# Eight kinds of small TensorE work start only when the last of them has its data: a two-layer encoder on one core

## The chip, the cores and the metric

One core of a Trainium2 chip runs the kernel. Its engines work side by side, each through its own instructions in a fixed order: TensorE (PE in the profile; its weight loads are PEld) multiplies matrices into PSUM, VectorE (DVE) and ScalarE (ACT) do elementwise work, and SyncE (SP) issues the transfers from memory. The metric is the device time of one execution in microseconds (us), as the median of several runs.

## The reference

Two layers work on x of 256 tokens by 2048 channels, in float32. Cut to what matters:

```python
shift, scale, gate = split(c @ w_ada + b_ada, 3)
h = rms_norm(x, g_pre) * (1 + scale) + shift
u, g_pool, q, k, v, g_diff = split(h @ w_in)            # 2048 -> 6144, six parts of 1024
pool = (trailing_mean(u, 2|4|8|16) - u) @ w_pool * pool_scale * silu(g_pool)   # 4 groups of 256
q, k = rotary(q), rotary(k)                              # 8 heads, 2 maps of 64 each
a = softmax(mask(q1 k1')) - lam * softmax(mask(q2 k2'))  # chunk-causal
diff = rms_norm(a @ v, subln_g) * (1 - lam_init) * silu(g_diff)
y = concat(pool, diff) @ w_out                           # 2048 -> 2048
x = x + (1 + gate) * rms_norm(y, g_post)
```

## The kernel before

**The two big products.** `h @ w_in` and `concat @ w_out` make up nearly all of TensorE's work. Each weight is split in two parts of lower precision, `whi` (a CAST on ACT) and `wlo` (the rest, a subtraction on DVE), and so is the activation (`hi` and `lo`). A product is the sum of three matmuls of 128x512: hi·whi, hi·wlo, lo·whi. In the profile these are the matmuls `accc<-whiz,hz`, `accc<-wloz,hz` and the same with `catz`; they are called the main matmuls below. A unit is one 256x512 piece of a weight: twelve main matmuls, six for each of its two 128-row halves. The tokens stand in two tiles of 128 (`st` 0 and 1). The order of the units, and so of all main matmuls, is laid out once in `plan` and `lay_out` (lines 438 and after) and does not depend on the scheduler.

**The small TensorE work.** Between the main matmuls TensorE does transposes and small products, all into PSUM tiles `psb`:

- `make_h` (line 912): for each 256 channels of a layer's input, ACT or DVE scales the two token tiles (`xn`, a `halfz` tile), four transposes of 128x128 turn them, and ACT and DVE write `hi` and `lo` (`hz`), which the main matmuls of w_in read.
- `rope` (line 1135): four transposes for each token tile of a finished q or k block.
- `head` and `heads` (lines 1163 and 1190): the score products of one head; the transposes of its softmax weights; the products with v; and four transposes of a pair of heads' gated result, which ACT and DVE turn into `catz`, read by the main matmuls of w_out.
- `pool_group` (line 1283): the products with a band matrix, and those with w_pool.

**What sets the order.** The program is written as many tasks (threads), one for each such piece of work; the main matmuls are a task of their own. Each instruction of a task asks for its engine, and a planner (`Flow`) picks which asking instruction is put on its engine next. It keeps a clock of its own for each engine and, for each tile, when it was written and last used. `depends` (line 276) gives the time at which all that an instruction reads is written. `next_of` (line 208) takes, among the instructions that could begin by now, the one with the earliest due time; the main matmuls have the latest due time of all, so any small TensorE instruction whose inputs have been ready long enough goes ahead of them. "Long enough" is `SLACK`, 1.5 us after its inputs are written (line 145); this counts for small TensorE work alone. When the task of the main matmuls waits for an `hz` or `catz` tile that no instruction makes yet, it does not ask, and TensorE gets whatever asks.

All this is settled while the program is built. On the chip each engine runs its list in order, and an instruction waits only for the tiles that it really reads or overwrites. So four transposes of one group are put on TensorE one by one: if the first two tiles are ready earlier than the last, main matmuls come between them.

`halfz`, `zz`, `yz`, `rawz`, `adaz` are tiles in SBUF (half tiles, block results, raw weights, rows of w_ada). Every instruction is recorded by one helper, so the profile shows line 126 for all of them; the tile names tell them apart.

Of the kernel before, what the change touches and what calls it, by code (L numbers as in the profile page):

```python
# [23 lines left out]
P = 128  # L24
# [59 lines left out]
class Task:  # L84
# [2 lines left out]

    def __init__(self, flow, f, due):
        self.flow, self.f, self.due = flow, f, due
        self.ask, self.cond, self.error, self.over = None, None, None, False  # L90
        self.go = threading.Semaphore(0)
        self.thread = threading.Thread(target=self.run, daemon=True)
        self.thread.start()
# [37 lines left out]
class Flow:  # L131
# [37 lines left out]

    def due(self, due):  # L170
        self.cur.due = due if callable(due) else lambda: due

    def resume(self, t):
        self.cur = t
# [73 lines left out]
    def turn(self, key, op, outs, ins, total, table):  # L248

        a = Ask()  # L250
        size = lambda x: math.prod(x.shape[1:])
        a.key, a.op, a.table, a.dma = key, op, table, "dma" in op
        a.bytes = 4 * size(outs[0]) * outs[0].shape[0]
        outs, ins = ([x for x in xs if not x.tensor.name.startswith(("in_", "out_"))] for xs in (outs, ins))
        a.outs, a.ins = [self.region(x) for x in outs], [self.region(x) for x in ins]
        a.names = {r[0] for r in a.outs + a.ins}
        a.dep, a.f32 = None, key == "tensor" and op == "matmul" and ins[-1].dtype == F32
        if a.dma:
            a.us = 0.35
        elif key == "tensor":  # L260
            n, dt = size(outs[0]), ins[-1].dtype
            if op == "transpose":
                a.us = 0.109
            elif dt == F32:
                a.us = max(0.109, 0.835e-3 * n) * (1 if ins[0].shape[0] == DQK else 2)
            else:
                a.us = 0.0135 + 0.4167e-3 * n if dt == F32R else 0.08
        else:
            fixed, each, accum, _ = self.COST[key]
            a.us = fixed + each * max(size(x) for x in outs + ins) + total * accum  # L270
            if key == "scalar":
                a.us += 0.07 * (len(ins) - 1)
        self.cur.ask = a
        self.pause()

    def depends(self, a):
        t = 0.0
        for r in a.ins:
            t = max(t, self.latest(self.wrote, r))
            if a.key != "tensor" and r[0].startswith(("acc", "ps")):  # L280
                t = max(t, self.latest(self.used, r))
        for r in a.outs:
            if a.key != "tensor" or not self.wrote.get(r[0]):
                t = max(t, self.latest(self.used, r))
        return t

    def note(self, a):
# [111 lines left out]
class Kern:  # L399
# [512 lines left out]
    def make_h(self, l, kp):  # L912

        nc, f = self.nc, self.f
        early = kp < self.START[l]

        f.wait(lambda: self.gated[l - 1][0] >= 2 and self.made[l] > 2 * kp + bool(early) if l else early or self.made[l] > 2 * kp)
        t, hi, lo = self.two("h")
        self.h[l, kp] = t, hi, lo
        if early:  # L920
            for st in range(NST):
                f.spawn(lambda st=st: self.half_h(l, kp, st, hi, lo), 2.0 * st + 0.1 * kp - 3.9 if l else st + 0.1 * kp - 5.5)
            return
        f.wait(lambda: all(r is not None for r in self.xr[l]))
        xn = self.tmp.take([P, NST, S], "xn")
        for st in range(NST):
            self.scaled(xn[:, st, :], self.x[st][:, kp * S : (kp + 1) * S], self.xr[l][st])
        b = self.bank()
        for i in range(2):
            for st in range(NST):  # L930
                nc.tensor.transpose(b[:, i * S + st * P : i * S + (st + 1) * P], xn[:, st, i * P : (i + 1) * P], self.ident)
        self.tmp.give(xn)
        hf = self.tmp.take([P, 2, S], "hf")
        for i in range(2):
            kt = 2 * kp + i
# [199 lines left out]
    def rope(self, l, nb, acc):  # L1135

        nc, v, f, z = self.nc, self.nc.vector, self.f, self.z[l, nb]
# [15 lines left out]
            rot.append(t1)  # L1153
        for st in range(NST):
            b, r = self.bank(), rot[st].rearrange("p g e d -> p (g e d)")
            for h in range(4):
                nc.tensor.transpose(b[:, h * P : (h + 1) * P], r[:, h * P : (h + 1) * P], self.ident)
            self.tmp.give(rot[st])
            self.copy(z[:, st, :], b)
            self.banks.give(b)  # L1160
        self.turning -= 1

    def head(self, l, h0, qT, kT, st, p):

        nc, v = self.nc, self.nc.vector
        c = slice(h0 * P, (h0 + 1) * P)
        nm, s = st[:, 0:4], st[:, 4:8]

        maps = [(m, slice(m * DQK, (m + 1) * DQK)) for m in range(2)]
        bank = self.banks.take([P, 512], "ps", n=2)  # L1170

        for t, o in ((0, slice(0, P)), (1, slice(P, 3 * P))):
            for m, r in maps:
# [16 lines left out]
    def heads(self, l, hp):  # L1190
# [34 lines left out]
        aT = []  # L1225
        for h in range(2):
            b = self.bank()
            for t in range(2):
                for j in range(t + 1):
                    nc.tensor.transpose(b[:, (t + j) * P : (t + j + 1) * P], p[h][t][:, 0, j * P : (j + 1) * P], self.ident)  # L1230
            if h == 0:
                self.tmp.give(tiles[0])
            a = self.tmp.take([P, 3, P], "aT")
            self.copy(a.rearrange("p i q -> p (i q)"), b[:, 0 : 3 * P])
            self.banks.give(b)
            aT.append(a)
        self.tmp.give(*tiles[1:])
        av = self.bank()
        for h in range(2):
            hs = slice((h0 + h) * P, (h0 + h + 1) * P)  # L1240
            o = av[:, 2 * h * P : (2 * h + 1) * P]
# [25 lines left out]

        cat, hi, lo = self.two("cat")
        b = self.bank()
        for i in range(2):  # L1270
            for st in range(NST):
                nc.tensor.transpose(
                    b[:, i * S + st * P : i * S + (st + 1) * P], gz[:, st, (h0 + i) * P : (h0 + i + 1) * P], self.ident
                )
# [8 lines left out]
    def pool_group(self, l, g):  # L1283
# [3 lines left out]
        u, gp = self.z[l, U[half]], self.z[l, GP[half]]  # L1287
        f.wait(lambda: self.band is not None and self.wps[l] is not None)
        b = self.bank()
        for ct in range(2):  # L1290
            c = slice((2 * gg + ct) * P, (2 * gg + ct + 1) * P)
            o = b[:, ct * S : (ct + 1) * S]
# [6 lines left out]
        self.copy(pt.rearrange("p c s -> p (c s)"), b)  # L1299
        self.banks.give(b)  # L1300
        m = self.bank()
        for dt in range(2):
            for ct in range(2):
                nc.tensor.matmul(
# [118 lines left out]
```

## Time and profile before

| what | value |
|---|---|
| median of 3 runs | 829.72 us (828.36 to 830.87) |
| the profiled execution | 828.36 us, of which the profile's span is 826.6 us |
| TensorE busy | 800.4 us, 97% of the span; 4058 matmuls |
| VectorE, ScalarE busy | 699.9 us (85%), 543.4 us (66%) |
| TensorE's granted clock | 0.996 of full speed over the span |
| HBM | 242.17 MB read, 296 GB/s over the span |

How to read what is quoted later: a row of the timeline gives start, length in us, engine, instruction, what it writes and reads, shapes and how often it stands there in a row; in brackets the idle time of the engine before it and what ended that idle time. Matmuls overlap each other, so the pitch of two matmuls is the difference of their starts, and not their length. A float32 matmul that is not a transpose has two records.

### The profile page before, as it was taken

The page shows a single profiled execution, that of the slowest core. Times are in us where ns is not written, and L with a number is a line of the kernel's source. Part 1 is how long each engine was busy: PE and PEld are TensorE (multiplying, and loading weights), DVE is VectorE, ACT ScalarE, POOL GpSimd, SP SyncE. Part 2 cuts the span into 40 slices and gives each one's busy share as a digit, 9 for nine tenths or more (in the row PEclk, how much of TensorE's full clock was granted, in tenths as well). Part 3 has the DMA queues.
Part 4 walks back from the last instruction along what each step waited for, and adds up shares of the span by engine and source line. Part 5 has one row for each costly group of instructions (what it writes and reads, how often), then busy time and mean ns, then how long its engine had stood idle before and what let it go on. Part 6 is the DMA issues. An engine that isn't in the chain of part 4 may idle for free.

```text
span 826.6 us, 11859 instructions
## 1 busy us (share of the span) xinstructions
PE 800.4 (97%) x4058; PEld 662.0 (80%) x4058; DVE 699.9 (85%) x1258; ACT 543.4 (66%) x944; POOL 0.2 (0%) x4
## 2 busy tenths in 40 slices
PE   4899999999999999999999999999999999999995
PEld 1688789888998877778878889888898887778884
DVE  7988998989989889888999979879788997678814
ACT  4879999967656666667387657576565466677520
POOL 0000000000000000000000000000000000000000
PEclk9999999999999999999999999999999999999998
DMA  9999999799999776876997899999999973545403
GB/s 344 407 409 409 408 408 334 277 357 380 364 404 337 262 237 204 300 230 209 313 340 264 312 338 360 341 357 364 330 404 374 380 256 112 183 142 170 134 0 102
DMA packets 68382, 245.07 MB, mean 296 GB/s; under 512 B 7745, under 2 KB 8033, under 8 KB 68065
## 3 DMA queue, kind: packets, MB, share of 16 engines
q1 hardware_dynamic: 68034, 244.14, 80.8%
q8 instruction: 32, 0.52, 0.3%
q10 hardware_dynamic: 288, 0.17, 0.1%
q14 instruction: 28, 0.23, 0.1%
HBM read 242.17 MB, written 2.11 MB: 296 GB/s over the span
## 4 chain that ended last, share of the span: by engine, by line
PE 94%; DVE 3%; ACT 2%; issue 0%; DMA 0%; DVEq 0%; ACTq 0%
PE accc L126 84%; PE psb L126 10%; DVE adaz L126 1%; ACT sqj L126 0%; ACT hz L126 0%; DVE x L126 0%; DVE rh L126 0%; DVE wloz L126 0%; DVE ry L126 0%; ACT zz L126 0%; PE accb L126 0%; ACT halfz L126 0%; ACT junkz L126 0%; DMA cb<-in_c 0%; ACT accc L126 0%
## 5 line engine op out<-in xcount | busy, mean ns | idle before, releaser
L126 PE MATMUL accc<-whiz,hz 128*128 128x512 f32 x1272 | 403.3, 394 | 7.6 <-ACT hz L126 5.3
L126 ACT CAST whiz<-rawz 128x1024 fp32r<-128x1024 f32 (+1 forms) x259 | 263.7, 1045 | 100.1 <-DMA rawz<-in_w_in 52.4
L126 DVE TENSOR_TENSOR wloz<-rawz,whiz 128x1024 fp32r<-128x1024 f32 (+1 forms) x259 | 307.2, 1207 | 14.3 <-ACT whiz L126 12.8
L126 PEld LDWEIGHTS accc<-whiz,hz 128*128 128x128 f32 x1272 | 237.9, 188 | 63.4 <-ACT hz L126 7.0
L126 DVE SCALAR_TENSOR_TENSOR adaz<-adaz,cb 128x1024 f32<-128x1024 f32 x192 | 231.5, 1220 | 30.3 <-DMA adaz<-in_w_ada 29.4
L126 PE MATMUL accc<-wloz,hz 128*128 128x512 f32 x636 | 249.6, 393 | 0.0
L126 PE MATMUL accc<-whiz,catz 128*128 128x512 f32 x512 | 165.7, 399 | 0.5 <-ACT catz L126 0.3
L126 PEld LDWEIGHTS accc<-wloz,hz 128*128 128x128 f32 x636 | 119.8, 188 | 24.6 <-DVE wloz L126 0.5
L126 PEld LDWEIGHTS accc<-whiz,catz 128*128 128x128 f32 x512 | 94.9, 188 | 20.7 <-ACT catz L126 0.7
L126 PE MATMUL accc<-wloz,catz 128*128 128x512 f32 x256 | 101.6, 397 | 0.0
L126 ACT COPY zz<-accc 128x512 f32<-128x512 f32 x128 | 73.9, 589 | 24.2 <-PE accc L126 23.6
L126 ACT COPY accc<-zz 128x512 f32<-128x512 f32 x110 | 65.1, 593 | 24.8 <-DVE halfz L126 17.8
L126 PE MATMUL accc<-hz,whiz 128*128 128x256 f32 x512 | 72.5, 284 | 0.0
L126 PEld LDWEIGHTS accc<-hz,whiz 128*128 128x128 f32 x512 | 66.7, 192 | 0.7
L126 PEld LDWEIGHTS accc<-wloz,catz 128*128 128x128 f32 x256 | 48.1, 188 | 10.4 <-issue 0.8
L126 PE MATMUL accc<-hz,wloz 128*128 128x256 f32 x256 | 41.2, 283 | 0.0
L126 ACT ACTIVATE sqj<-accc 128x512 bf16<-128x512 f32 x16 | 9.6, 600 | 41.0 <-PE accc L126 40.8
L126 PE MATMUL psb<-consts,halfz 128*128 128x128 f32 x176 | 30.6, 277 | 5.6 <-ACT halfz L126 5.6
L126 PEld LDWEIGHTS accc<-hz,wloz 128*128 128x128 f32 x256 | 35.3, 192 | 0.0
L126 DVE TENSOR_TENSOR yz<-accc,Gz 128x512 f32<-128x512 f32 x16 | 11.0, 690 | 27.8 <-ACT sqj L126 27.6
L126 PEld LDWEIGHTS psb<-consts,halfz 128*128 128x128 f32 x176 | 22.2, 142 | 14.1 <-ACT halfz L126 8.1
L126 ACT ACTIVATE halfz<-psb,sm 128x128 f32<-128x128 f32 (+1 forms) x64 | 26.4, 420 | 9.9 <-DVE sm L126 6.0
(108 smaller groups left out, 505.8 us busy)
## 6 DMA issues: line engine op xcount, KB each, us to landing
adaz<-in_w_ada SPq DMA_DIRECT2D x192, 512.0 KB, 7.1
rawz<-in_w_in SPq DMA_DIRECT2D x189, 512.0 KB, 7.1
rawz<-in_w_out SPq DMA_DIRECT2D x64, 512.0 KB, 4.2
x<-in_x SPq DMA_DIRECT2D x2, 1024.0 KB, 8.8
wpz<-in_w_pool SPq DMA_DIRECT2D x4, 512.0 KB, 7.2
Gz<-gate SPq DMA_DIRECT2D x4, 512.0 KB, 5.7
out<-x SPq DMA_DIRECT2D x8, 256.0 KB, 2.8
rawz<-in_w_in SPq DMA_DIRECT2D x6, 256.0 KB, 8.8
```

The source lines that it names most:

```text
L126: return f(*args, **kw)
```

## The change

The planner gets a call `until(*tiles)`: the next instruction of the task is held, in the planner's eyes, until these tiles are written too (`also`, read in `depends`). Eight places call it just before the first instruction of a group, with the tiles that the group's later instructions read: the four transposes of `make_h`, of `rope` and of a head pair's result, the score products, the transposes of the softmax weights, the products with v, and both products of a pool group. Nothing is added on the chip; no instruction and no wait is new. What changes is the order in which instructions are put on the engines, and with it which buffers they get.

```diff
--- before.py
+++ after.py
@@ -169,6 +169,10 @@
+    def until(self, *tiles):
+
+        self.cur.also = [self.region(x) for x in tiles]
@@ -253,7 +257,8 @@
         a.outs, a.ins = [self.region(x) for x in outs], [self.region(x) for x in ins]
-        a.names = {r[0] for r in a.outs + a.ins}
+        a.also, self.cur.also = self.cur.also, []
+        a.names = {r[0] for r in a.outs + a.ins + a.also}
@@ -282,6 +287,8 @@
             if a.key != "tensor" or not self.wrote.get(r[0]):
                 t = max(t, self.latest(self.used, r))
+        for r in a.also:
+            t = max(t, self.latest(self.wrote, r))
         return t
@@ -926,6 +933,7 @@
         b = self.bank()
+        f.until(xn)
         for i in range(2):
             for st in range(NST):
                 nc.tensor.transpose(b[:, i * S + st * P : i * S + (st + 1) * P], xn[:, st, i * P : (i + 1) * P], self.ident)
@@ -1153,6 +1161,7 @@
             b, r = self.bank(), rot[st].rearrange("p g e d -> p (g e d)")
+            f.until(r)
@@ -1162,12 +1171,13 @@
         bank = self.banks.take([P, 512], "ps", n=2)
+        f.until(qT, kT)
@@ -1225,6 +1235,7 @@
             b = self.bank()
+            f.until(*(p[h][t][:, 0, :] for t in range(2)))
@@ -1236,6 +1247,7 @@
         av = self.bank()
+        f.until(*aT, vz)
@@ -1267,6 +1279,7 @@
         b = self.bank()
+        f.until(gz[:, :, h0 * P : (h0 + 2) * P])
@@ -1287,6 +1300,7 @@
         b = self.bank()
+        f.until(u)
@@ -1303,6 +1313,7 @@
         m = self.bank()
+        f.until(pt)
```

Both programs have the same 3878 TensorE instructions. In the order before, main matmuls are interrupted by small work 114 times (from one instruction to eighteen at a time); in the changed order 93 times. Three places in detail, each as the order before and the changed order.

**First place: layer 0, the fourth h tile.** TensorE's order. `psb` is what the transposes of `make_h` write; `hz_1119` before and `hz_1142` now is the new h tile, and the matmuls above it read an older one. Before, one transpose of the group stands nine main matmuls higher up:

```order
L126 MATMUL accc_1128<-wloz_1095,hz_895 128x512
L126 MATMUL psb_1147<-consts_80,halfz_1120 128x128 x3
L126 MATMUL accc_1128<-whiz_1065,hz_895 128x512
L126 MATMUL accc_1139<-whiz_1065,hz_895 128x512
L126 MATMUL accc_1139<-wloz_1095,hz_895 128x512
L126 MATMUL accc_1139<-whiz_1065,hz_895 128x512
L126 MATMUL accc_1128<-whiz_1094,hz_1119 128x512
L126 MATMUL accc_1128<-wloz_1155,hz_1119 128x512
L126 MATMUL accc_1128<-whiz_1094,hz_1119 128x512
```

Now:

```order
L126 MATMUL accc_1145<-wloz_1078,hz_884 128x512
L126 MATMUL accc_1145<-whiz_1060,hz_884 128x512
L126 MATMUL psb_1157<-consts_80,halfz_1143 128x128 x4
L126 MATMUL accc_1130<-whiz_1070,hz_1142 128x512
L126 MATMUL accc_1130<-wloz_1101,hz_1142 128x512
L126 MATMUL accc_1130<-whiz_1070,hz_1142 128x512
L126 MATMUL accc_1145<-whiz_1070,hz_1142 128x512
L126 MATMUL accc_1145<-wloz_1101,hz_1142 128x512
```

Before, four main matmuls stand between the last transposes and the first matmul that reads the new tile. Now all four transposes stand together, directly ahead of that matmul.

ScalarE's order at the same place; `hz` is the rounded `hi` of each half of the new tile, `halfz` the unrounded value from which VectorE makes `lo`. Before:

```order
L126 ACTIVATE hz_1119<-psb_1147,AB_90 128x256
L126 ACTIVATE halfz_1171<-psb_1147,AB_90 128x256
L126 COPY zz_377<-accc_1099 128x512
L126 ACTIVATE hz_1119<-psb_1147,AB_90 128x256
L126 ACTIVATE halfz_1171<-psb_1147,AB_90 128x256
```

Now:

```order
L126 ACTIVATE hz_1142<-psb_1157,AB_90 128x256
L126 ACTIVATE halfz_1180<-psb_1157,AB_90 128x256
L126 CAST whiz_1136<-rawz_937 128x1024
L126 ACTIVATE hz_1142<-psb_1157,AB_90 128x256
L126 ACTIVATE halfz_1180<-psb_1157,AB_90 128x256
```

Between the first and the second half of the tile there was a COPY, and now there is a CAST of a weight.

**Second place: layer 0, the last pair of heads.** TensorE's order. `psb` is the transposed result of the pair, from which ScalarE and VectorE make `catz_3819` before and `catz_3834` now. Before:

```order
L126 MATMUL psb_3820<-consts_80,zz_527 128x128
L126 MATMUL accc_3249<-whiz_3463,catz_3675 128x512
L126 MATMUL psb_3820<-consts_80,zz_527 128x128 x2
L126 MATMUL accc_3249<-wloz_3491,catz_3675 128x512
L126 MATMUL psb_3820<-consts_80,zz_527 128x128
L126 MATMUL accc_3249<-whiz_3463,catz_3675 128x512
L126 MATMUL accc_3242<-whiz_3490,catz_3763 128x512
L126 MATMUL accc_3242<-wloz_3524,catz_3763 128x512
L126 MATMUL accc_3242<-whiz_3490,catz_3763 128x512
```

After these rows nine more matmuls read `catz_3763`, and the next reads `catz_3819`: thirteen main matmuls lie between the last transpose and the first use. Now:

```order
L126 MATMUL accc_3242<-whiz_3495,catz_3714 128x512
L126 MATMUL accc_3242<-wloz_3515,catz_3714 128x512
L126 MATMUL accc_3242<-whiz_3495,catz_3714 128x512
L126 MATMUL psb_3835<-consts_80,zz_527 128x128 x4
L126 MATMUL accc_3238<-whiz_3514,catz_3834 128x512
L126 MATMUL accc_3238<-wloz_3537,catz_3834 128x512
L126 MATMUL accc_3238<-whiz_3514,catz_3834 128x512
L126 MATMUL accc_3242<-whiz_3514,catz_3834 128x512
```

The four transposes stand together and directly ahead of the first matmul that reads what is made of them.

**Third place: layer 1, a change of accumulators near the end of w_in.** TensorE's order. `accc_6854` before and `accc_6844` now is an accumulator that is first filled by a COPY from an earlier sum. Before:

```order
L126 MATMUL accc_6801<-wloz_6569,hz_5698 128x512
L126 MATMUL accc_6801<-whiz_6554,hz_5698 128x512
L126 MATMUL psb_6849<-consts_80,halfz_6758 128x128 x4
L126 MATMUL psb_6862<-consts_80,halfz_6758 128x128 x4
L126 MATMUL accc_6854<-whiz_6567,hz_5698 128x512
L126 MATMUL accc_6854<-wloz_6577,hz_5698 128x512
L126 MATMUL accc_6854<-whiz_6567,hz_5698 128x512
```

Now:

```order
L126 MATMUL accc_6802<-wloz_6552,hz_5702 128x512
L126 MATMUL accc_6802<-whiz_6543,hz_5702 128x512
L126 MATMUL accc_6844<-whiz_6563,hz_5702 128x512
L126 MATMUL accc_6844<-wloz_6566,hz_5702 128x512
L126 MATMUL accc_6844<-whiz_6563,hz_5702 128x512
L126 MATMUL accc_6849<-whiz_6563,hz_5702 128x512
```

The eight transposes of a rotated block that stood ahead of the new accumulator's first matmul have moved to a later place. ScalarE's order there; before (the fill of `accc_6854` was a COPY on VectorE):

```order
L126 COPY zz_4823<-accc_6779 128x512
L126 COPY zz_4675<-psb_6849 128x512
L126 COPY zz_4675<-psb_6862 128x512
L126 COPY accc_6864<-zz_4895 128x512
L126 CAST whiz_6852<-rawz_6744 128x1024
```

Now:

```order
L126 COPY zz_4820<-accc_6774 128x512
L126 COPY accc_6844<-zz_4892 128x512
L126 COPY zz_4820<-accc_6802 128x512
L126 COPY accc_6849<-zz_4892 128x512
L126 CAST whiz_6842<-rawz_6777 128x1024
```

Both fills are now on ScalarE, in turn with the COPYs that empty the two accumulators before them.

More of the change, by code (lines that the diff above doesn't have):

```diff
@@ L89, in __init__ @@
         self.flow, self.f, self.due = flow, f, due
-        self.ask, self.cond, self.error, self.over = None, None, None, False
+        self.ask, self.cond, self.error, self.over, self.also = None, None, None, False, []
         self.go = threading.Semaphore(0)
@@ L1163, in head @@
     def head(self, l, h0, qT, kT, st, p):
-        nc, v = self.nc, self.nc.vector
+        nc, v, f = self.nc, self.nc.vector, self.f
         c = slice(h0 * P, (h0 + 1) * P)
```

## The prediction

> **What bounds the kernel now.** I read the page first (its engines and its chain), then the stretches of the span one by one, then the timeline at each place where TensorE waits.
>
> ```profile
> span 826.6 us, 11859 instructions
> PE 800.4 (97%) x4058; PEld 662.0 (80%) x4058; DVE 699.9 (85%) x1258; ACT 543.4 (66%) x944; POOL 0.2 (0%) x4
> PE 94%; DVE 3%; ACT 2%; issue 0%; DMA 0%; DVEq 0%; ACTq 0%
> ```
>
> TensorE sets the end: 97% busy, and 94% of the chain. Busy time does not tell where its 26 idle us lie, so the span is cut at the places where TensorE stops:
>
> ```profile
> 0.00:32.00 32.00, 18.25 (x40) 9.36 (x41) 24.91 (x87) 16.83 (x29) 0.20 (x4) 1.00 0.95 366
> 32.00:303.00 271.00, 270.20 (x1402) 228.88 (x1400) 246.39 (x365) 208.26 (x312) 0.00 (x0) 1.00 0.94 356
> 303.00:323.00 20.00, 19.28 (x98) 14.74 (x99) 16.58 (x34) 13.81 (x29) 0.00 (x0) 1.00 0.70 237
> 323.00:422.00 99.00, 99.00 (x500) 79.58 (x499) 89.16 (x216) 61.89 (x152) 0.00 (x0) 1.00 0.76 258
> 422.00:437.00 15.00, 14.18 (x63) 10.86 (x62) 13.98 (x35) 14.11 (x33) 0.00 (x0) 1.00 0.84 333
> 437.00:705.00 268.00, 268.00 (x1410) 228.94 (x1409) 233.79 (x345) 168.20 (x248) 0.00 (x0) 1.00 0.89 326
> 705.00:709.00 4.00, 3.65 (x20) 2.69 (x19) 2.73 (x7) 2.90 (x5) 0.00 (x0) 1.00 0.00 0
> 777.00:817.00 40.00, 39.88 (x177) 32.66 (x175) 12.52 (x23) 9.78 (x22) 0.00 (x0) 1.00 0.08 27
> ```
>
> The columns after each stretch are its length, then busy time and count of TensorE, its weight loads, VectorE, ScalarE and GpSimd, then granted clock, transfers' share and GB/s. Nearly all idle time lies in the first 32 us and after TensorE's last matmul at 817, and the change moves nothing there: by the order, the first TensorE instruction that moves is one that runs near 54 us, and behind the last moved transposes the main matmuls stand as before. Between 32 and 817 us TensorE is idle for some 2.7 us in all (0.80, 0.72, 0.82, 0.35 in the rows shown with gaps). So **what this change can win from waits is under 3 us; what it can lose has no such limit.** The last row gives the pitch of a main matmul, 39.88 / 177 = 0.225 us.
>
> **Part one: fewer interruptions.** A group taken apart, and one that stands whole:
>
> ```profile
> 85.20 0.40 PE L126 MATMUL accc<-wloz,hz 128*128 128x512 f32 x1
> 85.43 0.39 PE L126 MATMUL accc<-whiz,hz 128*128 128x512 f32 x1
> 85.66 0.27 PE L126 MATMUL psb<-consts,halfz 128*128 128x128 f32 x1
> 85.69 0.48 PE L126 MATMUL accc<-whiz,hz 128*128 128x512 f32 x1
> 86.01 0.49 PE L126 MATMUL psb<-consts,halfz 128*128 128x128 f32 x3
> 86.25 0.48 PE L126 MATMUL accc<-wloz,hz 128*128 128x512 f32 x1
> 86.57 0.39 PE L126 MATMUL accc<-whiz,hz 128*128 128x512 f32 x1
> ...
> 263.15 0.60 PE L126 MATMUL psb<-consts,halfz 128*128 128x128 f32 x4
> 263.51 0.48 PE L126 MATMUL accc<-wloz,hz 128*128 128x512 f32 x1
> 263.82 0.63 PE L126 MATMUL accc<-whiz,hz 128*128 128x512 f32 x2
> ```
>
> The whole group holds up the main matmuls by 0.36 us (263.15 to 263.51), and the matmul after it takes 0.31 us to the next instead of 0.225: 0.44 in all, 0.11 a transpose. Taken apart as one and three: from 85.20 to 86.57 it is 1.37 us, in which four main matmuls begin (4 x 0.225 = 0.90), so 0.47. Putting a group together is worth some 0.025 us. The order has 114 interruptions before and 93 after: 21 x 0.025 = **-0.5 us**. Bounds: nothing, or the whole late matmul saved each time, 21 x 0.085 = -1.8. I stay at the low end, since the two cases above are direct measurements of the exchange.
>
> [...]
>
> **Part two: groups that now stand directly ahead of their reader.** This is where I expect the loss. The wait in the planner's eyes holds the first transposes back until the last tile is written plus its 1.5 us of slack. Where that moment is late, the group drops down to the first main matmul that needs its result, and everything from the transpose to the written tile lies open. Behind the waiting main matmul all TensorE work is queued.
>
> First place (fourth h tile of layer 0). Before:
>
> ```profile
> 111.68 0.49 PE L126 MATMUL psb<-consts,halfz 128*128 128x128 f32 x3
> 112.20 0.57 ACT L126 ACTIVATE hz<-psb,AB 128x256 fp32r<-128x256 f32 x1 [0.95 <-PE psb L126]
> 113.17 0.40 PE L126 MATMUL accc<-wloz,hz 128*128 128x512 f32 x1
> 113.26 0.43 DVE L126 TENSOR_TENSOR hz<-halfz,hz 128x256 fp32r<-128x256 f32 x1 [0.57 <-ACT halfz L126]
> 113.74 0.74 PE L126 MATMUL accc<-whiz,hz 128*128 128x512 f32 x2 [0.18 <-DVE hz L126]
> 114.32 0.40 PE L126 MATMUL accc<-wloz,hz 128*128 128x512 f32 x1
> ```
>
> From the start of the three transposes the `hi` half is written 112.77 - 111.68 = 1.09 us later, and the matmul that reads `lo` starts 2.06 us later. A fourth transpose adds 0.11 to both: 1.20 and 2.17. Before, four main matmuls covered the first of these and the wait was for `lo` alone: 113.17 to 113.74 is 0.57, less 0.225, so 0.34, and the matmul after a wait is 0.11 late as well (113.74 to 114.32 is 0.58 for two). Now, counted from the group's start: without a wait the main matmuls go on at 0.36; they go on at 1.20, a loss of 0.84 and 0.11. The third of them, which reads `lo`, could start at 1.20 + 0.34 + 0.225 = 1.77 and waits until 2.17: 0.40 and 0.11. Together 1.46, less the 0.45 lost there before, less the 0.085 that follows any group: +0.9. Then the second half: ScalarE has a CAST ahead of it where it had a COPY of 0.59 us:
>
> ```profile
> L126 ACT CAST whiz<-rawz 128x1024 fp32r<-128x1024 f32 (+1 forms) x259 | 263.7, 1045 | 100.1 <-DMA rawz<-in_w_in 52.4
> L126 DVE TENSOR_TENSOR wloz<-rawz,whiz 128x1024 fp32r<-128x1024 f32 (+1 forms) x259 | 307.2, 1207 | 14.3 <-ACT whiz L126 12.8
> ```
>
> The CAST's mean is 1045 ns, so 1.05 - 0.59 = 0.46 later, with little room: +0.4. In sum **+1.3 us**; bounds +0.5 (VectorE ready at once and the second half hidden) and +1.9 (both halves open).
>
> Second place (last head pair of layer 0):
>
> ```profile
> 383.76 0.27 PE L126 MATMUL psb<-consts,zz 128*128 128x128 f32 x1
> 384.07 0.69 ACT L126 ACTIVATE catz<-psb,cols 128x512 fp32r<-128x512 f32 x1 [2.72 <-PE psb L126]
> 384.80 0.75 DVE L126 SCALAR_TENSOR_TENSOR catz<-psb,cols,catz 128x512 fp32r<-128x512 f32 x1 [1.32 <-ACT catz L126]
> ```
>
> From the last transpose `hi` takes 384.76 - 383.76 = 1.00 us and `lo` 1.79. Before, thirteen main matmuls (2.9 us) hid both. Now none does: the fourth transpose starts 0.33 after the first, so `hi` is there at 1.33 and `lo` at 2.12 (and 0.05 to the matmul). Loss: 1.33 - 0.36 = 0.97; the third matmul could start at 1.33 + 0.34 + 0.225 = 1.90 and waits 0.27; two late matmuls, less the one that any group has: 0.14. **+1.4 us**; bounds +1.0 (`lo` hidden) and +1.9 (the four transposes also wait for VectorE, by one of its 0.43 us steps or so).
>
> The other groups keep their cover: by the order the last pairs of layer 1 stand 14 and 16 main matmuls ahead of their readers (over 3 us against 2.2), the later h tiles 20 or more.
>
> **Part three: what else moves.** The rotated block of the third place goes away from a change of accumulators that it covered. There were such changes with and without cover:
>
> ```profile
> 303.07 0.50 PE L126 MATMUL accc<-whiz,hz 128*128 128x512 f32 x1 [0.68 <-ACT accc L126]
> 304.21 0.50 PE L126 MATMUL accc<-whiz,hz 128*128 128x512 f32 x1 [0.18 <-ACT accc L126]
> ...
> 706.99 0.50 PE L126 MATMUL accc<-whiz,hz 128*128 128x512 f32 x1
> 708.30 0.50 PE L126 MATMUL accc<-whiz,hz 128*128 128x512 f32 x1 [0.35 <-ACT accc L126]
> ```
>
> The changed order at 707 has the form of the one at 303: both fills on ScalarE between two COPYs. So 0.68 + 0.18 in place of 0.35: **+0.5 us**, from 0 to +0.6.
>
> A gain: two waits for pool tiles go away.
>
> ```profile
> 320.59 0.50 PE L126 MATMUL accc<-whiz,catz 128*128 128x512 f32 x1 [0.25 <-ACT catz L126]
> 321.97 0.73 PE L126 MATMUL accc<-whiz,catz 128*128 128x512 f32 x2 [0.21 <-DVE catz L126]
> ```
>
> In the changed order the second half of layer 0's pool work stands some 80 main matmuls ahead of its reader: 0.25 + 0.21 = **-0.5 us**, up to -0.7 with the late matmuls behind them.
>
> At nothing I cost the new order of the transfers on SyncE and of the weight splits on ScalarE and VectorE. Transfers fill 94% of the stretch from 32 to 303 us and TensorE is still busy for 270.20 of 271.00; and in both orders all but fifteen to twenty of the 512 weight tiles, most of them at the start, are written twelve or more main matmuls (2.7 us) ahead of their use. Without that cover a CAST and its subtraction would lie open, over 2 us a unit.
>
> **The sum.** -0.5 + 1.3 + 1.4 + 0.5 - 0.5 = +2.2 us. The profiled execution took 828.36 us, 1.8 around its span, so 830.6; it was the fastest of the three, 1.36 under their median of 829.72. On the median's scale the forecast is **831.9 us**, 0.27% up. What a measurement can tell from no change is about 0.3%, 2.5 us: the forecast is a small loss just under that.
>
> **Rivals.**
>
> - *Forecast*: 831.9, chance 0.40. All terms but the first are sequences that the trace shows, laid bare; with all terms at their bounds the sum is between -1.0 and +3.9.
> - *Slower: VectorE is late at the two laid-bare groups.* The planner's clock says that the tiles are written 1.5 us before the group. VectorE is busy 246.39 of 271 us in the first place's stretch. If it runs two weight subtractions behind the planner (2 x 1.207 = 2.4 us), 0.9 us comes on top at each place: +4.0, 833.7. It decides from 0.3 us more than the sum. For it: nothing fills TensorE meanwhile. Against it: before, the stretch from 323 to 422 us, where most such groups stand, has no idle time at all. 0.37.
> - *Slower: a lone transpose is cheaper than one in a group.* If only the 0.03 us at 85.66 counted, each healed split would cost 0.11 - 0.03 = 0.08 more: +1.7 instead of -0.5, 834.1. Against it stands the late matmul at 86.01. 0.05. [...]
> - *It does nothing that counts*: TensorE is held in the planner's eyes alone, many head groups still come apart, and the losses at their lower ends (0.5 + 1.0) nearly cancel with the gains (0.5 + 0.7): +0.3, 830.0. 0.10.
> - *Faster*: each healed split saves its whole late matmul (-1.8), the pool waits go (-0.7), and the laid-bare groups find their tiles early enough to cost nothing: 827.2. The rows of the second place leave hardly any room for that. 0.08.
>
> Within 0.3%: 0.40 + 0.10 = 0.50; slower: 0.37 + 0.05 = 0.42; faster 0.08. The range takes in the cancelling case and the slower ones, 828.2 to 834.8; the forecast's own is 830.0 to 833.5.
>
> **What would show it.** Part one: whole groups of four at 0.44 us each, and TensorE's interruptions fewer without a visible drop of its time. Part two: TensorE idle by some 0.9 us and then 0.3 us before `accc<-whiz,hz` near 113 us, ended by ScalarE and VectorE, and the same before `accc<-whiz,catz` near 387 us. Part three: two waits for ScalarE near 707 us, none near 321. The forecast is wrong if the stretches from 32 to 422 us and from 437 to 777 us do not get longer by about these amounts, or if a wait over 1.5 us stands at a place not named here.

## The result and the profile after

The changed kernel takes 834.73 us (median of 21 runs, 831.29 to 841.25), the kernel before 830.38 in runs beside it (21 runs, 828.36 to 833.82). The ratio is 1.0053, with a 95% interval of 1.0038 to 1.0069: **slower by 4.4 us**. A second set of runs gave 834.82 (12 runs) and 1.0060 (1.0039 to 1.0081). The forecast was 831.9, 2.8 us too low, and the case that it held for likeliest ("within 0.3%") lost to the next one. The range, 828.2 to 834.8, holds the time at its upper edge.

The profiled execution of the change took 838.01 us, 3.3 above its median. Its page (the span, the engines, the chain):

```profile
span 835.9 us, 11856 instructions
PE 805.0 (96%) x4058; PEld 664.4 (79%) x4058; DVE 701.1 (84%) x1258; ACT 545.2 (65%) x944; POOL 0.2 (0%) x4
PE 77%; DVE 5%; DMA 4%; ACT 2%; issue 1%; DVEq 0%; SPq 0%; ACTq 0%
```

And TensorE's waits by what ended them, with total, times and longest:

```profile
PE psb L126 <- ACT zz L126: 2.3, 2, 1.7
PE accc L126 <- ACT accc L126: 1.7, 4, 0.7
PE accc L126 <- DVE hz L126: 1.4, 5, 0.6
PE accc L126 <- ACT catz L126: 0.8, 1, 0.8
PE accc L126 <- DVE wloz L126: 0.3, 1, 0.3
```

In this trace's chain, the share of TensorE falls from 94 to 77%: the work that ended last now passes through transfers and VectorE on its way. (The chain of a second trace, used below, covers only a quarter of its span and can't be set beside this one.) The wait for `ACT zz` stood in no row before. The places of the forecast, in TensorE's timeline of the change, with one that it did not name (83.46) at the top:

```profile
83.46 0.50 PE L126 MATMUL accc<-wloz,hz 128*128 128x512 f32 x1 [0.32 <-DVE wloz L126]
...
115.44 0.50 PE L126 MATMUL accc<-whiz,hz 128*128 128x512 f32 x1 [0.66 <-ACT hz L126]
116.36 0.73 PE L126 MATMUL accc<-whiz,hz 128*128 128x512 f32 x2 [0.18 <-DVE hz L126]
118.22 0.73 PE L126 MATMUL accc<-whiz,hz 128*128 128x512 f32 x2 [0.18 <-DVE hz L126]
...
387.85 0.60 PE L126 MATMUL psb<-consts,zz 128*128 128x128 f32 x4
389.22 0.50 PE L126 MATMUL accc<-whiz,catz 128*128 128x512 f32 x1 [0.78 <-ACT catz L126]
389.56 0.40 PE L126 MATMUL accc<-wloz,catz 128*128 128x512 f32 x1
390.01 0.73 PE L126 MATMUL accc<-whiz,catz 128*128 128x512 f32 x2
390.58 0.39 PE L126 MATMUL accc<-wloz,catz 128*128 128x512 f32 x1
...
715.11 0.50 PE L126 MATMUL accc<-whiz,hz 128*128 128x512 f32 x1 [0.67 <-ACT accc L126]
716.24 0.50 PE L126 MATMUL accc<-whiz,hz 128*128 128x512 f32 x1 [0.17 <-ACT accc L126]
718.75 0.50 PE L126 MATMUL accc<-whiz,catz 128*128 128x512 f32 x1 [0.17 <-DVE zz L126]
```

Both kernels run the same 3456 main matmuls in the same order, so the start of the same matmul can be compared in the traces. The stages end where the small work done is the same again (start times of the records; gain or loss in us against the one trace of before):

| stage of the change, us | first trace | second trace | forecast |
|---|---|---|---|
| start to 41 | +1.4 | 0.0 | 0 |
| to 122 (first place) | +1.6 | +1.6 | +1.3 |
| to 418 (heads and pool of layer 0) | -0.2 | -0.4 | +0.9 and its part of -0.5 |
| to 439 (between the layers) | 0.0 | +0.7 | 0 |
| to 648 | +1.0 | +0.6 | 0 |
| to 687 (**pool groups of layer 1**) | **+4.4** | +0.7 | 0 |
| to the end | +1.1 | +2.1 | +0.5 |
| sum | +9.3 | +5.4 | +2.2 |

The trace of before is the fastest execution of its set (828.36 us, 2.0 under that set's median), so the second trace of the change, at 834.02 us, is the fair one to set beside it. The 1.4 us at the start are eight main matmuls at half rate, in one trace of the change and not in the other; the waits just before them (1.25 and 0.20 us) stand in the trace of before too, with nothing slow behind them (see the last section).

**The largest term of the first trace is the one that the forecast said would prove it wrong: a wait over 1.5 us at a place not named.** Near 653 us TensorE waits before the band products of the first pool group of layer 1, and then runs slowly:

```profile
653.68 0.51 PE L126 MATMUL psb<-band,zz 128*128 128x144 f32 x2 [1.65 <-ACT zz L126]
654.82 3.09 PE L126 MATMUL psb<-band,zz 128*128 128x128 f32 x14 [0.62 <-ACT zz L126]
...
649.75 1.05 ACT L126 CAST whiz<-rawz 128x1024 fp32r<-128x1024 f32 x1 [1.57 <-DVE wloz L126]
652.10 1.04 ACT L126 CAST whiz<-rawz 128x1024 fp32r<-128x1024 f32 x1 [1.29 <-DVE wloz L126]
653.05 0.58 ACT L126 COPY zz<-accc 128x512 f32<-128x512 f32 x1
654.18 0.58 ACT L126 COPY zz<-accc 128x512 f32<-128x512 f32 x1
```

These are rows of the timeline, TensorE's first and then ScalarE's. ScalarE copies the accumulator into `zz` (the pool's `u`) in its own order, and two weight casts stand ahead of the copy. Each of them waits, by the profile, for a subtraction on VectorE. Transfers are full at that time (share 0.99), and after the wait the granted clock is about halved (columns as in the prediction, with the clock 0.52 in the second row):

```profile
640.00:653.00 13.00, 12.03 (x54) 9.62 (x52) 10.58 (x14) 6.62 (x8) 0.00 (x0) 1.00 0.99 388
655.20:658.60 3.40, 3.40 (x16) 3.21 (x16) 2.73 (x4) 2.23 (x4) 0.00 (x0) 0.52 0.97 365
```

So 2.3 us of waiting cost some 4 us. How often that happens was the first question.

### The profile page after: what moved, and what is told of

It is laid out like the page before. It is cut to its first block, busy times and chain, and to the rows that moved or that the text cites. A ratio compares the mean times of both kernels' runs of the same rounds, so it can differ in the third digit from the quotient of the medians.

```text
span 835.9 us, 11856 instructions
## 1 busy us (share of the span) xinstructions
PE 805.0 (96%) x4058; PEld 664.4 (79%) x4058; DVE 701.1 (84%) x1258; ACT 545.2 (65%) x944; POOL 0.2 (0%) x4
## 4 chain that ended last, share of the span: by engine, by line
PE 77%; DVE 5%; DMA 4%; ACT 2%; issue 1%; DVEq 0%; SPq 0%; ACTq 0%
PE accc L126 68%; PE psb L126 9%; DMA rawz<-in_w_in 4%; DVE wloz L126 2%; DMA adaz<-in_w_ada 1%; DVE x L126 1%; DVE adaz L126 1%; ACT whiz L126 1%; ACT zz L126 0%; ACT sqj L126 0%; DVE rh L126 0%; DVE ry L126 0%; ACT accc L126 0%; DVE yz L126 0%; ACT halfz L126 0%
## 5 line engine op out<-in xcount | busy, mean ns | idle before, releaser
L126 PEld LDWEIGHTS accc<-wloz,catz 128*128 128x128 f32 x256 | 48.1, 188 | 10.2 <-issue 1.1
L126 PE MATMUL psb<-consts,halfz 128*128 128x128 f32 x176 | 28.1, 276 | 5.6 <-ACT halfz L126 5.6
```

Source lines behind the costliest of these rows:

```text
L126: return f(*args, **kw)
```

## The experiments

Eleven kernels, each in runs beside the kernel before on the same chip. Medians in us, ratio to before with its 95% interval:

| kernel | median (runs) | ratio |
|---|---|---|
| the change again | 834.82 (12) | 1.0060 (1.0039 to 1.0081) |
| fourth h tile due earlier | 832.70 (12) | 1.0020 (1.0003 to 1.0037) |
| without the pool's wait | 832.38 (12) | 1.0017 (1.0000 to 1.0034) |
| all groups split | 877.50 (6) | 1.0563 (1.0528 to 1.0598) |
| all h groups laid bare | 857.03 (4) | 1.0304 (1.0267 to 1.0341) |
| all gated groups laid bare | 841.82 (4) | 1.0132 (1.0110 to 1.0155) |
| whole score groups alone | 825.83 (9) | 0.9940 (0.9919 to 0.9962) |
| the change, score groups whole | 827.45 (7) | 0.9949 (0.9929 to 0.9969) |
| the same without the pool's wait | 826.24 (6) | 0.9947 (0.9928 to 0.9965) |
| the same with all h tiles due earlier | 828.34 (12) | 0.9964 (0.9948 to 0.9981) |
| whole score groups, fourth h tile earlier | 824.75 (6) | 0.9926 (0.9903 to 0.9949) |

### The change again

> The changed kernel once more, for a second trace and a second interval. The forecast's places (near 113, 387, 707 us) must show the same waits of 0.6 to 0.8 us and then 0.05 to 0.2 us. Open is the wait of 1.65 and 0.62 us that the first trace shows before the band products at 653.68 us (ScalarE's copy of zz late), which the forecast did not name. If it belongs to the order, it stands in this trace too, within some 0.5 us of that length, and so do the slow main matmuls behind it (0.42 us apart instead of 0.225). If it was an accident of that one execution, it is gone or under 0.5 us, and the time is 831 to 835 us either way. Ratio to before: 1.003 to 1.007.

The waits at the forecast's places come back to the hundredth (0.66, 0.18, 0.18; 0.78, 0.05; 0.67, 0.17). The one before the band products is shorter, and nothing runs slowly behind it:

```profile
651.50 1.89 PE L126 MATMUL psb<-band,zz 128*128 128x128 f32 x14 [0.47 <-ACT zz L126]
653.15 0.48 PE L126 MATMUL accc<-whiz,hz 128*128 128x512 f32 x1
```

It is neither fixed nor gone: the same order met it with 2.3 us in one execution and 0.5 in the next. Places that hang on TensorE's own timing repeat; this one hangs on when weights land: the two casts ahead of ScalarE's work for this stage waited 3.70 and 1.41 us for transfers in the first trace, 3.93 and 0.21 us in the second.

### Two places uncovered, one due time

```diff
-                f.spawn(lambda l=l, kp=kp: self.make_h(l, kp), self.need_h(l, kp, 4.0))
+                f.spawn(lambda l=l, kp=kp: self.make_h(l, kp), self.need_h(l, kp, 6.0 if (l, kp) == (0, 3) else 4.0))
```

> The changed kernel, with the fourth h tile of layer 0 due 6 instead of 4 us ahead of its first reader. In the order this gives back the four main matmuls between the group's last transpose and its reader (first place), and the last head pair's group (second place) gets its cover too. Theory of the forecast: the two places cost 1.3 and 1.4 us, so this is 2.7 us faster than the changed kernel (ratio to it 0.9967), near 832 us where that one takes 834.7, with no waits near 387 us and one of under 0.5 us near 113 us. Rival (the two places are not where the time went, but waits elsewhere such as the one at 653 us): within 1 us of the changed kernel.

It is 2.1 us under the changed kernel by the medians, 3.3 by the two ratios, where 2.7 was expected and under 1 by the rival; the intervals of the two ratios stand barely apart (up to 1.0037, from 1.0039). The trace has 0.17 us near 114 and nothing near 387 us. Part of the gain is paid back: four waits for pool tiles between 314 and 328 us (1.75 us in all; before the change there were two, 0.46 us in all), and 1.3 and 0.6 us before the band products.

### Without the pool's wait

```diff
         b = self.bank()
-        f.until(u)
         for ct in range(2):
```

> The changed kernel without the wait for all of u ahead of the band products of the pool groups; all else of the change is kept. By the order the first band group of layer 1 stands six main matmuls earlier, as before the change, and layer 0's last head pair gets seven main matmuls of cover. Theory that the wait at 653 us comes from the change's pool part: it is gone here, and with it and the slow matmuls behind it some 4 us, and 1.4 us of the second place: 829 to 830 us. Rival (ScalarE's casts run late there because the weights land late, whatever the pool groups do): the wait stays within 1 us, and only the second place's 1.4 us goes: 833 us.

832.38: nearer to the rival (833) than to the theory (829 to 830). In this trace the wait before the band products is gone, but one trace proves little here. Two later kernels without that wait for `u` in their band products say more: their traces have 1.14 us and 1.03 us at this place, the latter again with a late cast ahead of the copy:

```profile
644.65 0.76 PE L126 MATMUL psb<-band,zz 128*128 128x144 f32 x4 [1.03 <-ACT zz L126]
...
643.07 1.05 ACT L126 CAST whiz<-rawz 128x1024 fp32r<-128x1024 f32 x1 [1.29 <-DVE wloz L126]
644.02 0.58 ACT L126 COPY zz<-accc 128x512 f32<-128x512 f32 x1
```

So the wait can come without the pool's `until`. It is ScalarE's copy behind late casts, and other shifts of the order lay it bare too. Whether the `until` makes it longer or more frequent stays open: of seven traces with it, four show a wait here (1.65 and 0.62, 1.32 and 0.62, 0.62, 0.47 us), of six without it two; the waits of over 1.2 us are all among the former. It would take many more traces to tell.

### The price of an interruption

```diff
+        if k == "tensor" and self.small:
+            for due, at, us, t in rows:
+                if due > 1e8 and at <= t0:
+                    return t, at
```

`small` says that the last TensorE instruction noted was not a main matmul.

> The changed kernel, with a rule that lets a main matmul go ahead after every small TensorE instruction wherever one is ready: 380 interruptions in place of 93, with the same 422 small instructions. This measures the price of an interruption, which the forecast put at 0.025 us from two rows: 287 x 0.025 = +7 us against the changed kernel. If a lone transpose has its weight load hidden and costs 0.03 us instead of 0.11, it gets faster by up to 287 x 0.08 = 23 us. If every interruption costs the whole 0.085 us of the late matmul behind it, it is 24 us slower. Up to 2 us more may come from groups that end later, two or three main matmuls ahead of their readers.

It is 42.7 us slower than the changed kernel: none of the three. First the transposes, in TensorE's timeline of this kernel:

```profile
810.69 0.39 PE L126 MATMUL accc<-wloz,catz 128*128 128x512 f32 x1
810.92 0.27 PE L126 MATMUL psb<-consts,halfz 128*128 128x128 f32 x1
810.95 0.48 PE L126 MATMUL accc<-whiz,catz 128*128 128x512 f32 x1
811.26 0.27 PE L126 MATMUL psb<-consts,halfz 128*128 128x128 f32 x1
811.29 0.48 PE L126 MATMUL accc<-whiz,catz 128*128 128x512 f32 x1
811.61 0.27 PE L126 MATMUL psb<-consts,halfz 128*128 128x128 f32 x1
811.64 0.48 PE L126 MATMUL accc<-wloz,catz 128*128 128x512 f32 x1
811.95 0.63 PE L126 MATMUL accc<-whiz,catz 128*128 128x512 f32 x2
```

From 810.69 to 811.95 are 1.26 us with four main matmuls (0.90): 0.12 us for each lone transpose. Each looks free at its start (0.03 us to the next matmul) and is paid for by the matmul behind it. By the start times of all records, a group of four taken fully apart costs 0.473 us (22 such groups, middle value) and a whole one 0.455 (26 groups of the second trace): **0.006 us for each further interruption**, not 0.025. The products on the pool's weights cost 0.21 us a record either way, the band products 0.12.

The scores are another matter. A head's six products use 64 rows of the array each, two and two on different halves. In the trace of before, a group that comes apart as one and five:

```profile
288.69 0.61 PE L126 MATMUL accc<-whiz,hz 128*128 128x512 f32 x2
289.24 0.48 PE L126 MATMUL psb<-zz,zz 64*128 64x128 f32 x2
289.65 0.50 PE L126 MATMUL accc<-wloz,hz 128*128 128x512 f32 x1
289.99 0.63 PE L126 MATMUL accc<-whiz,hz 128*128 128x512 f32 x2
290.54 0.70 PE L126 MATMUL psb<-zz,zz 64*128 64x128 f32 x5
291.08 0.22 PE L126 MATMUL psb<-neg,ind 64*128 64x128 bf16 x1
291.09 0.38 PE L126 MATMUL psb<-zz,zz 64*128 64x256 f32 x1
291.30 0.22 PE L126 MATMUL psb<-neg,ind 64*128 64x128 bf16 x1
291.45 0.50 PE L126 MATMUL accc<-wloz,hz 128*128 128x512 f32 x1
```

Inside the group, records on the two halves start together (291.08 and 291.09 here; 0 to 7 ns apart by the records). The lone one at 289.24 has no partner and takes 0.41 us, with a late matmul on either side. By the records it costs 0.62 us, the five behind it 1.11, and a whole group of six 1.12: **a score group in two costs 0.61 us more**. In the fully split kernel the score groups take 53.6 us in place of some 25; those 28 us, 7.8 us more waiting and some 6 us lost in two half-rate stretches behind the longest waits (10.2 us from 401.9 and 6.8 us from 821.7 on, some 11.5 of them busy) are nearly all of the 42.7.

Main matmuls fill all 128 rows, each loads its own weights for 0.19 us (PEld is busy for 664.4 of 835.9 us in the page above), and still they begin 0.225 us apart: these loads run beside matmuls on the same rows, and so does that of a lone transpose. In the trace of before:

```profile
85.20 0.40 PE L126 MATMUL accc<-wloz,hz 128*128 128x512 f32 x1
85.20 0.19 PEld L126 LDWEIGHTS accc<-whiz,hz 128*128 128x128 f32 x1
...
85.43 0.39 PE L126 MATMUL accc<-whiz,hz 128*128 128x512 f32 x1
85.44 0.14 PEld L126 LDWEIGHTS psb<-consts,halfz 128*128 128x128 f32 x1
85.66 0.27 PE L126 MATMUL psb<-consts,halfz 128*128 128x128 f32 x1
```

Why a lone transpose costs 0.12 us all the same is not shown.

### The score groups whole

The change waits for `qT` and `kT`. The second product also needs the second bank, which can come free later; so 12 of 16 groups still came apart after it, 13 before.

```diff
-        f.until(qT, kT)
+        f.until(qT, kT, *bank)
...
-            t = max(t, self.latest(self.wrote, r))
+            t = max(t, self.latest(self.used if r[0].startswith("ps") else self.wrote, r))
```

First in the kernel before, with no other `until`:

> The kernel before, with one wait of the change's kind alone: a head's six score products begin only when qT and kT are written and both of their banks are free (the change waits for qT and kT, not for the second bank). By the order all 16 groups are whole; before, 13 of 16 begin with one product alone and four others (five with the mask's) come later. In the split groups' trace and in that of before a lone score product costs 0.62 us and the rest 1.11, while a whole group costs 1.12. If that price is right, this is 13 x 0.61 = 7.9 us faster than before: near 822 us, ratio 0.990. Rival (the price of an interruption is the same for all kinds, 0.005 to 0.025 us): no difference that can be measured, 829.5 to 830.5.

825.83, 4.8 us under before (interval 3.2 to 6.7): the rival falls. TensorE does get the 7.9 us: by the records, its time in small work falls from 81.0 to 73.1 us. Some of it is given back between the layers, where TensorE now arrives earlier than its operands. Its timeline there:

```profile
425.81 1.09 PE L126 MATMUL psb<-consts,halfz 128*128 128x128 f32 x4 [2.53 <-ACT halfz L126]
```

The stretch that begins there, with the granted clock at 0.54:

```profile
425.80:429.50 3.70, 3.69 (x11) 2.91 (x12) 3.62 (x7) 3.49 (x10) 0.00 (x0) 0.54 1.03 409
```

In before the wait at this place was 0.75 us, with no half-rate stretch: 1.8 and some 1.7 us of the gain.

Then in the changed kernel, and there without the pool's wait:

> The changed kernel, in which the wait of the score products takes in their second bank. All 16 groups whole in the order, 12 of 16 in two in the changed kernel. By the 0.61 us per group: -7.3 us. Against that the order lays the last head pair of layer 1 directly ahead of its reader (+1.4 by the price of the second place) and gives three main matmuls of cover to that of layer 0 (-0.7): some 828 us, 6.6 us under the changed kernel. Rival (one price for all): 834 to 836.

> As the one before, without the wait for u ahead of the band products. In the order both last head pairs keep their cover, and the band products of layer 1 stand where they stood before the change; the first place (h tile near 113 us) stays laid bare. From the run without the pool's wait (832.4) less 11 or 12 groups x 0.61 us: 825 to 826 us, with no wait near 650 us. Rival: 831 to 833.

827.45 (expected 828) and 826.24 (expected 825 to 826): the price holds within the changed kernel too, 7.4 us and 6.1 us under the kernels that differ only in this. The two last head pairs wait for 0.78 and 0.90 us where the order leaves them bare.

> As the one before, with all h tiles due 6 us ahead of their readers instead of 4. By the order the first place gets its four main matmuls of cover back: 1.3 us less, 824 us, with one wait under 0.4 us near 113 us. If more tiles early only hold buffers and push weight casts back, waits for weights appear and it is not faster than the one before (825 to 826).

828.34, not faster: waits for weight subtractions appear (0.32 and 0.63 us at 83 and 92 us), as the second alternative had it, and the pool tiles' waits near 315 to 329 us (2.4 us) come back.

### The price of a group without cover

```diff
+        f.wait(lambda: self.at >= self.first_use["w_in", l, kp].step)
         b = self.bank()
         f.until(xn)
```

> The changed kernel, in which every whole h tile's transposes are held back until the main matmuls stand at their first reader: 13 groups stand directly ahead of their readers, against one in the changed kernel. This measures the price of the first place twelve times more. By the forecast's term of 1.3 us each: 12 x 1.3 = +16 us against the changed kernel, 850 us, with waits of some 0.7 us for ScalarE and 0.2 for VectorE at each. By its lower bound (0.5): +6; by the upper (1.9): +23. The rival that VectorE is late at such places (0.9 us more at each) would give 12 x 2.2 = +26 us, 861.

By the ratios it is 20 us over the changed kernel (2.4%), 1.7 us a group, and by the medians 1.9: above the term of 1.3, under the rival's 2.2. The term of 1.3 is the wrong measure here: from it the forecast had deducted 0.45 us that the first place lost already before the change, and these groups had lost nothing. With them put back the forecast's own working gives 1.75 a group, +21 us. By start times, seven of the 13 groups cost 1.4 to 1.8 us more than a covered one, three 2.1 to 2.4, and three some 5; that the total still comes out at 20 to 22 is partly luck, since several waits of the changed kernel (the second place's among them) are not in this trace. An ordinary place and one of the three:

```profile
143.85 0.50 PE L126 MATMUL accc<-whiz,hz 128*128 128x512 f32 x1 [0.66 <-ACT hz L126]
...
614.45 0.50 PE L126 MATMUL accc<-whiz,hz 128*128 128x512 f32 x1 [2.83 <-ACT hz L126]
...
612.89 1.04 ACT L126 CAST whiz<-rawz 128x1024 fp32r<-128x1024 f32 x1 [1.64 <-DVE adaz L126]
613.84 0.56 ACT L126 ACTIVATE hz<-psb,AB 128x256 fp32r<-128x256 f32 x1
```

Where ScalarE is free, the wait is 0.66 us (and 0.18 us for VectorE two matmuls later); where its next instruction is a cast that has to wait itself, the group stands behind it (2.5 to 2.8 us at three places, each with a half-rate stretch after it). The rival had the right kind of trouble on the wrong engine.

```diff
+        f.wait(lambda: self.at >= self.first_use["w_out", l, 4 + hp].step)
         b = self.bank()
         f.until(gz[:, :, h0 * P : (h0 + 2) * P])
```

> The same for the head pairs' gated tiles: all eight groups stand directly ahead of their readers in place of one. By the forecast's term of 1.4 us (bounds 1.0 and 1.9): 7 x 1.4 = +10 us against the changed kernel, 845 us, with a wait of 0.8 us for ScalarE at each and hardly any for VectorE. With VectorE late by 0.9 us at each: +16, 851. The order also gives up the wait for the last pool group here, so up to 1 us less.

841.82: 7 us over the changed kernel for seven groups, 1.0 each (0.5 to 1.2 by the two intervals), at the lower bound of the term. That is a net figure: waits of 1.7 us that the second trace of the change has between 686 and 715 us are not in this one (the expectation allowed for 1 us of that kind). Seven of the eight show 0.78 us for ScalarE and at most 0.06 for VectorE; one has 1.33 and 0.33. By start times, the group and the eight main matmuls behind it cost 1.84 to 1.86 us in the six places where nothing else comes between, in place of 0.48 for a covered group: **1.36 us a group**, the term itself.

### A version that beats both

> The kernel before, with whole score groups (as in the run that had these alone) and the fourth h tile of layer 0 due 2 us earlier; nothing else of the change. By the order all 16 score groups are whole and that h tile has over eight main matmuls of cover, where before it had four and a wait of 0.18 us. Expected 0.2 to 0.3 us under the run with the score groups alone, so 825.5 us, ratio 0.994; if the earlier tile pushes weight casts back, waits for weights near 80 to 120 us appear and it is 827.

824.75 us, ratio 0.9926 (0.9903 to 0.9949), 10 us under the changed kernel. A wait for a weight subtraction did appear (0.91 us at 114 us), as the second alternative had it. Its interval overlaps with that of the score groups alone, so only these are shown to make it fast.

## Why the prediction was right or wrong

- **Part one (-0.5): the sum came near, the working did not.** The price of an interruption was read from two cases with 0.025 us between them. It is 0.006 for transposes, so the interruptions gave -0.1, and 0.61 for score groups, of which one fewer is split: -0.6 (an estimate; no run changes these alone). The step that failed is "21 x 0.025": one price for all kinds, from transposes alone. Had the score groups been looked at, the forecast would have seen that the change leaves 12 of 16 in two.
- **Rival "a lone transpose is cheaper than one in a group" (0.05)**: refuted at over 150 of them: 0.12 us each, against 0.11 in a group. The late matmul behind each takes the gain back, as the row at 86.01 had said. That its time (834.1) is the nearest to the result is luck.
- **First place (+1.3)**: +1.24 and +1.26 us in the two traces. The profile shows the wait for `hi` as 0.66 and not as some 0.9, because it counts idle time from the end of the last transpose; by start times the reader begins 1.25 us after the group in place of 0.36, so 0.89 against the forecast's 0.84. Right.
- **Second place (+1.4)**: the bracketed waits, 0.78 and 0.05, look smaller than the forecast's 0.97 and 0.27, for the same reason. By start times the reader begins 1.37 us after the group (387.85 to 389.22), a loss of 1.01; the third matmul is 0.22 late (389.56 to 390.01 less 0.225). From 387.85 to 390.58 are 2.73 us with four main matmuls (0.90), less the 0.44 of a covered group: +1.39; against the same matmuls of before it is +1.3 in both traces. Right, and the bare groups of the last run but one give the same.
- **Part three (+0.5) and the pool waits (-0.5)**: 0.67 + 0.17 in place of 0.35, and no wait left near 321 us. Right.
- **"At nothing I cost the new order of the transfers ... and of the weight splits"**: this is the step that failed. It checked how far weights are written ahead of their matmuls. It did not check what else stands behind the casts on ScalarE: the copies of accumulators that band products read at once. It also passed over the fifteen to twenty weights with little cover, of which one is now late (83.46, 0.4 us in both traces). With the waits near 508 us (0.6 to 1.0) and before the band products (0.7 to 4.4) that makes 1.7 us in the second trace and 5.8 in the first; the median lacks 2.8. The range holds the result, but at its upper edge and for a reason that none of its cases had: that is in part luck.
- **Rival "VectorE is late at the two laid-bare groups"**: its time (833.7) comes within 1.1 us of the result, but not for its reason: VectorE ended 0.05 and 0.18 us after the need. ScalarE's queue is what comes late, elsewhere.
- In the last stage, beside part three, a wait of 0.17 us at 718.75 and (in the second trace alone) one of 0.73 us for an accumulator at 686.69 are new; some 0.4 us of it is assigned to no row.

## What to carry to other kernels

Price an interruption by kind: a group whose members share the array at the same time loses far more by coming apart (0.61 us for six score products) than a row of transposes (0.006 us for each further interruption), and a rule that holds a group until its inputs are written must take in its output banks too. A group that was put off cost no more than any other (0.48 us for a head pair) while main matmuls stood between it and its reader; without them it cost the whole way from TensorE through ScalarE and back (1.36 us more for a head pair, 1.4 to 1.8 for seven of the 13 h tiles), plus whatever stood ahead of it in ScalarE's queue (waits of 2.5 to 2.8 us at the three h tiles behind a late cast). When an order is moved, check each engine's queue for short copies that TensorE reads at once and that stand behind long work which waits for transfers (in the first trace, casts that had waited 3.70 and 1.41 us for transfers, and then 1.65 us of waiting on TensorE).

## What the runs showed of the hardware

- **In these traces half rate came in whole stretches of 3.41 us, and it mattered where a wait fell.** In the thirteen traces, between 24 us and TensorE's last matmul, the granted clock drops to half eleven times (in the first trace of the change at 30.67 and 655.31 us, in that of before not once). Each time it stays there for 3.41 us, or two or three times that, and all of a trace's changes lie multiples of 3.41 us apart. Main matmuls then stand 0.43 us apart instead of 0.225, so a stretch costs up to 1.7 us. In these traces the drops go with TensorE's idle time within the 3.41 us stretch before. The first trace of the change (two rows) and that of before (two rows) have the same waits there, 1.25 us (ending at 28.80 and at 29.02) and 0.20 us:

```profile
27.30:30.70 3.40, 1.94 (x7) 0.96 (x6) 2.63 (x10) 2.66 (x7) 0.00 (x0) 1.00 1.03 410
30.70:34.10 3.40, 3.40 (x9) 2.62 (x9) 3.40 (x5) 3.40 (x7) 0.00 (x0) 0.50 1.03 412
25.00:28.40 3.40, 2.58 (x9) 1.58 (x9) 3.12 (x11) 2.77 (x5) 0.00 (x0) 1.00 1.03 408
28.40:31.80 3.40, 2.58 (x9) 1.66 (x10) 2.73 (x7) 3.29 (x7) 0.00 (x0) 1.00 1.03 410
```

  In the change both fall into one stretch (1.46 us idle), and half rate follows; in before the longer one lies across the border of two (0.82 us idle in each), and nothing follows. Of the stretches at full rate in all traces, the seven with 1.94 us or more of idle time were all followed by half rate, four of the ten with 1.44 to 1.76 us, and none with less; what decides in between is not shown. So the same two waits cost their own length in one execution and some 1.4 us more in the other.
- **Products on different halves of the array ran side by side**: their records start 0 to 7 ns apart, and a lone score product cost 0.62 us, a whole group of six 1.12.
